# Loading pages one or two steps before their use in a fused two-block kernel

## The chip, the cores and the metric

The kernel runs on one core of a Trainium2 chip, as one program. The metric is device time in microseconds (us) of one execution, from which a median over several runs is taken. All loops are unrolled when the program is built.

## What is computed

The input is 256 tokens of width 2048 (`x`), 256 memory tokens (`mem`), 256 context tokens (`ctx`) and two conditioning vectors (`c`, `c_ctx`). Two blocks follow each other. The first block:

```
mem_n = rmsnorm(mem, mem_norm_g)
x = retention_layer(x, norm_a, w_in_a, w_mem_kv[0], w_out_a, mem_n)
kv = shared_kv(x, kv_norm_g, w_kv)
x = dilated_layer(x, norm_b, w_in_b, w_mem_kv[1], w_out_b, mem_n, kv)
x = rmsnorm(x, final_norm_g)
```

Both layers also attend to the memory through `mem_n @ w_mem_kv[layer]`. The second block has two layers, a sliding-window attention (swa) and a latent attention (mla), each with a modulation:

```
shift, scale, gate = split(silu(c) @ ada_w[i] + ada_b[i], 3)       # the same with c_ctx for ctx
h  = rmsnorm(x, norm_g[i]) * (1 + scale) + shift
hc = rmsnorm(ctx, norm_g[i]) * (1 + scale_c) + shift_c
o, oc = mixer(h, hc, ...)
x, ctx = x + gate * o, ctx + gate_c * oc
```

All arrays are float32. The change alters none of this arithmetic.

## The kernel before

**Projections.** Nearly all time goes into matrix products of 256 or 512 tokens with weight matrices. Every operand is split into a high part in the matmul's own float32 type and a low part (what the rounding left), and three products are summed: high by high, low by high, high by low. A projection (`gemm`, `gemm_T`, `gemm_wide`, `gemm_HL`) makes one block of 512 output columns (1024 in `gemm_wide`), and walks the contraction in steps `u` of four 128-row pieces. A step is one call of `wload`: a weight load of 1 MB into a `raw` buffer (four of them), a cast to `wh` on ScalarE (line 134, three buffers) and a subtraction to `wl` on VectorE (line 135, two buffers); then its matmuls (line 99) follow. `gemm_HL` fills four PSUM accumulators of the five that exist; `add_halves` evacuates them by a copy on ScalarE (line 300) and an addition on VectorE (line 301). There are 32 such evacuations.

**Side work.** Behind the matmuls of each step stand two calls. `tick()` advances every spawned generator by one `yield`: small jobs such as norms, attention chains and loads are written as generators and so spread over the steps of the projections; `later(fn, wait)` runs `fn` after `wait` more ticks, and `drain()` runs all to their end. `fill(n)` adds `n` to a credit, and for each whole credit takes the next of 96 modulation units (`ada_unit`): one load of 1 MB of `ada_w` into a `raw` buffer and eight VectorE instructions (lines 383 and 385), with a transposition and sums (388, 389) after every fourth. `FA`, `FB`, `FS` are the credits per step in the retention, dilated and swa layers; what is left before the last swa column block is done by `fill(96)`.

**Order.** All loads and stores are issued by one queue, SP (line 96). Tiles come from pools; nearly all activations live in pages of 128 by 512 float32 from one pool of 66 pages. The order of instructions on each engine is not the text's: a planner in the framework sets it when the program is built, by the text's order as priority, by its own estimate of durations, and by when buffers come free. Each engine then works through its list in that order.

**The places that the change touches.**
- `mem_rows` (line 605) loads the eight row pages of `mem` in four steps, and sums their squares (`rows`, `sumsq`, line 123); then come the reciprocal root, the conditioning vectors and a broadcast. `enter_x` (616) follows: in each of four steps it loads two transposed pages of `x`, scales them into the pages `ha` (`split_gain`, lines 319 and 320), loads two row pages and sums their squares. All this runs beside the two `gemm_HL` projections of `mem_kv(1)` (four steps each, first memory projections) and the first of `mem_kv(0)`.
- `enter_ctx` (905) does the like for `ctx`, beside the column blocks 1 to 3 of the dilated layer's output projection (six steps each), into the pages `hs`.
- The first swa projection (`kr`, line 1019) starts with two steps for the context tokens (`ahead=2`), before the latent tokens are normed, modulated and transposed by `hT_mod` (lines 895, 111, 332, 339, 340). The norm needs the last block of the output projection (additions in lines 944 and 946, small VectorE sums, a power on GpSimd in line 961).
- In the swa layer the mixed heads of the first two groups are spilled to DRAM (`mixsd`, eight pages) and brought back by `reload` (1052), spawned before the last `gemm_T`; each page is loaded into `mixSL`, cast to `mixSH` (line 325) and subtracted in place (line 326). The swa output projection `out_swa` then begins with these pages.

Of the kernel before, what the change touches and what calls it, by code (L numbers as in the profile page):

```python
# [11 lines left out]
F32 = mybir.dt.float32  # L12
# [6 lines left out]
P = 128  # L19
D = 2048  # L20
NK = D // P
# [1 line left out]
S128 = 128 ** -0.5  # L23
NPAGES = 66
NRAW = 4
FA, FB, FS = 0.25, 0.23, 0.58
NMISC = 3
MPER = 2

# [31 lines left out]
def tile_kernel(ctx: ExitStack, tc: tile.TileContext, d, out):  # L61
# [17 lines left out]
    def pg(s="pg", dt=F32, shape=None):  # L79
        return ppool.tile(shape or [P, 512], dt, name=nm(s), tag="pg")  # L80
# [14 lines left out]
    def load(dst, src):  # L95
        nc.sync.dma_start(dst, src)
# [24 lines left out]
    def sumsq(dst, src, w):  # L121
        j = spool.tile([P, 512], BF16, name=nm("junk"), tag="junk", bufs=1)
        A.activation(j[:, :w], src, AF.Square, accum_out=dst)
# [37 lines left out]
    def later(fn, wait=0):  # L161
        def gen():
            for _ in range(wait):
                yield
            fn()
            return
            yield
        spawn(gen())
# [11 lines left out]
    def gemm(act, tl, w, nkk, c0, ncols=512, nfill=0.0, order=None, pre=None, mid=False, ahead=0, apart=False):  # L180


        accs = [acc() for _ in tl]
        order = list(range(0, nkk, 4)) if order is None else order
        order = [q if isinstance(q, tuple) else (q, min(4, nkk - q)) for q in order]
        first, last = order[0][0], sum(order[-1]) - 1
        tl = [(act, t) if act else t for t in tl]
        held = {}

        def products(u, n, sel, tick_mid):  # L190
            h, l = held[u]
            for k in range(n):
                for i in sel:
                    sh, sl = tl[i][0].st(u + k, tl[i][1])
                    mm(accs[i][:, :ncols], sh, h[:, k], u == first and k == 0, False)
                    mm(accs[i][:, :ncols], sl, h[:, k], False, False)
            if tick_mid:
                tick()
            for k in range(n):
                for i in sel:  # L200
                    mm(accs[i][:, :ncols], tl[i][0].st(u + k, tl[i][1])[0], l[:, k], False, u + k == last)

        for u, n in order[:ahead]:
            held[u] = wload(w, u * P, n, c0, ncols)
            products(u, n, range(2), False)
        for i, (u, n) in enumerate(order):
            if pre:
                pre(u)
            if i < ahead:
                products(u, n, range(2, len(tl)), mid)  # L210
            else:
                held[u] = wload(w, u * P, n, c0, ncols)
                if apart and u + n == nkk:
                    for j in range(len(tl)):
                        products(u, n, [j], False)
                else:
                    products(u, n, range(len(tl)), mid)
            tick()
            fill(nfill)
        return accs  # L220
# [91 lines left out]
    def split_gain(act, kk, src, gcol, t0=0, nt=None):  # L312

        h, l = act.sl(kk) if isinstance(act, ActHL) else act.sl(kk, t0, nt)
        if gcol is None:
            A.copy(h, src)
            V.tensor_tensor(l, src, h.bitcast(F32), ALU.subtract)
        else:
            A.activation(h, src, AF.Copy, scale=gcol)
            V.scalar_tensor_tensor(l, src, gcol, h.bitcast(F32), ALU.mult, ALU.subtract)  # L320
# [28 lines left out]
    def gain(i, kk):  # L349
        return gT[:, i * NK + kk : i * NK + kk + 1]  # L350

    N_A, N_B, KV_N, MEM_N, N20, N21 = range(6)
# [226 lines left out]
    ha = new_HL("ha")  # L579
# [4 lines left out]
    def enter_page(srcT, act, gi, i):  # L584
        u = pg("natT")
        load(u, srcT[i])
        for k in range(2):
            split_gain(act, 2 * i + k, u[:, k * 256 : (k + 1) * 256], gain(gi, 2 * i + k))

    def enter(srcT, act, gi, c):  # L590
        for i in (2 * c, 2 * c + 1):
            enter_page(srcT, act, gi, i)

    def rows(src, q, c):
        for t in range(2):
            u = pg("nat")
            load(u, src[t * P : (t + 1) * P, c * 512 : (c + 1) * 512])
            sumsq(q[:, 4 * t + c : 4 * t + c + 1], u, 512)

    def row_rsqrt(dst, q):  # L600
        ssq = small(2)
# [2 lines left out]

    def mem_rows():
        q = const([P, 8], "ssm")
        for c in range(4):
            rows(d["mem"], q, c)
            yield
        row_rsqrt(memr, q)  # L610
        condition()
        yield
        bcast_rows(memrB[:, 0:256], memr)
        yield from enter_x()

    def enter_x():
        q = const([P, 8], "ssxa")
        for c in range(4):
            enter(d["xT"], ha, N_A, c)
            rows(d["x"], q, c)  # L620
            yield
        row_rsqrt(ra, q)
        V.tensor_scalar(sra, ra, 1.0 / 16.0, None, ALU.mult)
        V.tensor_scalar(hra, ra, 0.5, None, ALU.mult)
# [3 lines left out]
    def mem_kv(layer):  # L628
        kT, vn = [None] * 4, [[None] * 2 for _ in range(2)]
        w = d["w_mem_kv"][layer]  # L630
        if layer == 1:
            accs = gemm_wide(hm, w, 1024, [(0, 1), (1, 1)] + [(u, 2) for u in range(2, NK, 2)],
                             lambda u: u % 2 == 0 and enter_page(d["memT"], hm, MEM_N, u // 2))
            spawn(mem_rows())
            vs = [[pg("mkv") for _ in range(2)] for _ in range(2)]
            for c in range(2):
                for t in range(2):
                    A.copy(vs[c][t], accs[c][t])

            def post():  # L640
                for c in range(2):
                    for t in range(2):
                        A.activation(vs[c][t], vs[c][t], AF.Copy, scale=memr[:, t : t + 1])
                        load(memb[4 + 2 * t + c], vs[c][t])
            later(post, 7)
        for c in range(2):
            raw = add_halves(gemm_HL(hm, w, c * 512, FA if layer == 0 or c else 0), "mkT")

            def post(c=c, raw=raw):
                for j in range(2):  # L650
                    V.tensor_tensor(raw[j].rearrange("p (k n) -> p k n", k=2), raw[j].rearrange("p (k n) -> p k n", k=2),
                                    bc(memrB[:, 0:256], 2), ALU.mult)
                    if layer == 1:
                        load(memb[2 * c + j], raw[j])
                    else:
                        kT[2 * c + j] = split_page(raw[j], "mkTs")
            later(post, 5 if layer == 1 and c == 0 else 0)
        if layer == 0:
            for c in range(2):
                acs = gemm(hm, [0, 1], w, NK, 1024 + c * 512, nfill=FA)  # L660
                for t in range(2):
                    vn[t][c] = split_rows(acs[t], memr[:, t : t + 1])
        return kT, vn
# [27 lines left out]
    for hg in range(2):  # L691
        dec = []
        for h in range(4):
            q = pg("dec")
# [64 lines left out]
    for c in range(4):  # L759
        res = []  # L760
        for t in range(2):
            q = pg("xr")
# [125 lines left out]
    hs = new_act(NK, 512, "hs")  # L888
# [15 lines left out]

    def enter_ctx():
        q, rc = const([P, 8], "ssc"), const([P, 2], "rc")
        for c in range(4):
            rows(d["ctx_2"], q, c)
        row_rsqrt(rc, q)
        yield  # L910
        rcB = pg("rcB")
        bcast_rows(rcB[:, 0:256], rc)
        for i in range(8):
            u = pg("natT")
            load(u, d["ctxT"][i])
            V.tensor_tensor(u.rearrange("p (k n) -> p k n", k=2), u.rearrange("p (k n) -> p k n", k=2),
                            bc(rcB[:, 0:256], 2), ALU.mult)
            split_mod(hs, 2 * i, 2, u, modA[0][:, 1, 2 * i : 2 * i + 2], adaT[0][:, 2 * i : 2 * i + 2, 1])
            if i % 2:
                yield  # L920

    def splitB(u):
        if u == 12:
# [8 lines left out]
    for c in range(4):  # L932
# [3 lines left out]
        for t in range(2):  # L936
            q = pg("x1r")
# [4 lines left out]
        for t in range(2):  # L942
            q = res[t]
# [21 lines left out]
    WS = d["swa_w_in_2"]  # L965
    TL = [2, 3, 0, 1]
# [45 lines left out]
    def evac4(acs):  # L1012
        res = [None] * 4
        for i, t in enumerate(TL):
            res[t] = pg("ev")
            A.copy(res[t], acs[i])
        return res

    kr = evac4(gemm(hs, TL, WS, NK, 2048, nfill=FS,
                    pre=lambda u: hT_mod([z[0][u // 4], z[1][u // 4]], r23, 0, 0, hs, u // 4), ahead=2))  # L1020
    kn = [None] * 4
    for t in TL:
# [27 lines left out]
            mixS.H[k], mixS.L[k] = pg("mixSH", F32R), pg("mixSL", F32R)  # L1050

    def reload():
        for u in range(0, 8, 4):
            for k in range(u, u + 4):
                open_page(k)
                q = mixS.L[k].bitcast(F32)
                load(q, mixsd[k])
                split_in_place(mixS, k)
            yield

    for j in range(4):
        qr = evac4(gemm(hs, TL, WS, NK, j * 512, nfill=FS))
# [506 lines left out]
```

## Time and profile before

| | us |
|---|---|
| median of 3 runs | 3096.49 (3095.86 to 3096.86) |
| profiled execution | 3096.07 |
| its span, first to last instruction | 3094.3 |
| TensorE busy | 3042.5 (98%) |
| VectorE busy | 2163.8 (70%) |
| ScalarE busy | 1411.2 (46%) |

The profile is of one execution. Busy time of TensorE (PE) is the time in which some matmul is in flight. The granted clock of a stretch is given as a share of 2.4 GHz; 1.0 is that level and 0.5 is 1.2 GHz, so a value between them is a mixture. Idle time of an engine is listed with the instruction that ended it. A DMA's time runs from its issue on SP to its landing.

### The profile page before, as it was taken

What the parts mean: (1) busy time and instruction counts of PE and PEld (TensorE: products, weight loads), DVE (VectorE), ACT (ScalarE), POOL (GpSimd) and SP (SyncE); (2) the same over time, 40 slices, a digit from 0 to 9 for tenths busy, and PEclk for the clock granted to TensorE, in tenths of its full rate; (3) what the DMA queues carried; (4) which work ended last, traced back from release to release, by engine and by line L of the source; (5) the groups of instructions that cost most, each with busy time, mean ns of one, the idle gap of its engine ahead of it and who ended that gap; (6) DMA issues with size and microseconds to landing.
All of it is one profiled execution on the core that took longest, in us unless ns stands there. A gap on an engine that the chain in (4) does not pass through costs nothing.

```text
span 3094.3 us, 38864 instructions
## 1 busy us (share of the span) xinstructions
PE 3042.5 (98%) x15386; PEld 2570.2 (83%) x15386; DVE 2163.8 (70%) x3277; ACT 1411.2 (46%) x1870; POOL 86.2 (3%) x63
## 2 busy tenths in 40 slices
PE   9799999999999999999999999999999999999999
PEld 7688888888888888888888888788888778888887
DVE  5677877878867767766766747867676766656774
ACT  6444444445433433433433555424355342645662
POOL 0000000000000000000000000010110100000110
PEclk9899999999999999999999999999999999999999
DMA  8776676677566656656656667544433435453234
GB/s 307 242 243 226 210 245 222 221 260 264 206 208 234 232 185 227 222 195 227 231 191 227 222 224 248 181 157 156 136 118 108 163 103 180 145 176 123 69 103 129
DMA packets 307863, 600.77 MB, mean 194 GB/s; under 512 B 12896, under 2 KB 24800, under 8 KB 307680
## 3 DMA queue, kind: packets, MB, share of 16 engines
q1 hardware_dynamic: 307680, 598.29, 57.3%
q8 instruction: 120, 1.97, 0.3%
q14 instruction: 63, 0.52, 0.0%
HBM read 585.62 MB, written 12.62 MB: 193 GB/s over the span
## 4 chain that ended last, share of the span: by engine, by line
PE 92%; DVE 4%; DMA 1%; ACT 1%; POOL 1%; issue 1%; SPq 0%; DVEq 0%; ACTq 0%
PE acc L99 83%; PE pT L111 2%; PE so L99 1%; PE bs L99 1%; PE ls L99 1%; PE bo L99 1%; DMA raw<-in_ada_w 1%; DVE wl L135 1%; PE xs L99 1%; DVE ada L385 1%; PE lo L99 1%; PE mixT L111 0%; PE mo L99 0%; PE ms L99 0%; PE yT L111 0%
## 5 line engine op out<-in xcount | busy, mean ns | idle before, releaser
L135 DVE TENSOR_TENSOR wl<-raw,wh 128x2048 fp32r<-128x2048 f32 (+2 forms) x437 | 982.2, 2248 | 601.8 <-PE acc L99 343.4
L134 ACT CAST wh<-raw 128x2048 fp32r<-128x2048 f32 (+2 forms) x437 | 821.0, 1879 | 1136.3 <-PE acc L99 1021.0
L385 DVE SCALAR_TENSOR_TENSOR ada<-raw,condth,ada 128x512 f32<-128x512 f32 x720 | 496.0, 745 | 60.7 <-DMA raw<-in_ada_w 60.5
L99 PE MATMUL acc<-hb,wh 128*128 128x512 f32 x896 | 232.6, 393 | 0.0
L99 PE MATMUL acc<-wh,ha 128*128 128x512 f32 x896 | 215.2, 392 | 0.0
L99 PE MATMUL acc<-hk,wh 128*128 128x512 f32 x768 | 199.4, 394 | 0.1
L99 PEld LDWEIGHTS acc<-wh,ha 128*128 128x128 f32 x896 | 166.3, 188 | 33.5
L99 PE MATMUL acc<-wh,hk 128*128 128x512 f32 x768 | 185.3, 393 | 0.0
L99 PEld LDWEIGHTS acc<-hb,wh 128*128 128x128 f32 x896 | 159.8, 188 | 27.0 <-DVE hb L443 0.5
L99 PEld LDWEIGHTS acc<-wh,hk 128*128 128x128 f32 x768 | 143.1, 188 | 28.6
L99 PEld LDWEIGHTS acc<-hk,wh 128*128 128x128 f32 x768 | 136.7, 188 | 22.5 <-DVE bq L301 0.4
L99 PE MATMUL acc<-wh,hsH 128*128 128x512 f32 x384 | 151.2, 397 | 0.0
L99 PE MATMUL acc<-wh,hsL 128*128 128x512 f32 x384 | 150.6, 395 | 0.0
L99 PEld LDWEIGHTS acc<-hb,wl 128*128 128x128 f32 x896 | 126.1, 190 | 11.8 <-ACT hb L442 0.2
L99 PE MATMUL acc<-hb,wl 128*128 128x256 f32 x896 | 129.8, 282 | 0.0
L99 PEld LDWEIGHTS acc<-hk,wl 128*128 128x128 f32 x768 | 108.0, 190 | 10.2
L99 PE MATMUL acc<-hk,wl 128*128 128x256 f32 x768 | 110.9, 282 | 0.0
L99 PE MATMUL acc<-wl,ha 128*128 128x512 f32 x448 | 110.7, 389 | 0.0
L99 PE MATMUL acc<-wh,mixSH 128*128 128x512 f32 x256 | 101.2, 400 | 5.8 <-ACT mixSH L325 3.8
L99 PE MATMUL acc<-wh,mixSL 128*128 128x512 f32 x256 | 101.0, 400 | 2.2 <-DVE mixSL L326 2.2
L99 PE MATMUL acc<-hsH,wh 128*128 128x512 f32 x256 | 99.7, 391 | 0.0
L99 PE MATMUL acc<-hsL,wh 128*128 128x512 f32 x256 | 99.3, 390 | 0.0
(404 smaller groups left out, 5405.1 us busy)
## 6 DMA issues: line engine op xcount, KB each, us to landing
raw<-in_ada_w SPq DMA_DIRECT2D x96, 1024.0 KB, 5.1
raw<-in_w_kv SPq DMA_DIRECT2D x96, 1024.0 KB, 5.0
raw<-in_w_in_b SPq DMA_DIRECT2D x80, 1024.0 KB, 5.0
raw<-in_w_in_a SPq DMA_DIRECT2D x64, 1024.0 KB, 5.3
raw<-in_swa_w_in SPq DMA_DIRECT2D x40, 1024.0 KB, 5.0
raw<-in_w_mem_kv SPq DMA_DIRECT2D x31, 1024.0 KB, 5.3
raw<-in_w_out_a SPq DMA_DIRECT2D x24, 1024.0 KB, 5.2
raw<-in_w_out_b SPq DMA_DIRECT2D x24, 1024.0 KB, 5.2
```

Of the source, the lines that this page charges most:

```text
L99: T.matmul(o, lhsT=l, rhs=r, start=start, stop=stop)
L111: T.transpose(o, i, ident[:k, :k])
L134: A.copy(h, rw)
L135: V.tensor_tensor(l, rw, h.bitcast(F32), ALU.subtract)
L385: V.scalar_tensor_tensor(a[ci], raw[:, k, :], col, a[ci], ALU.mult, ALU.add)
```

## The change

A helper `staged(n, begin, end, lag)` runs `begin(i)` in one tick and `end(i)` `lag` ticks later, so that up to `lag` further groups are begun before a group's work. Memory and `x` are staged by two steps, the context rows by one, the context pages by two (one page per tick in place of two), the spilled pages by one (in two groups of four). `mem_rows` thereby takes two ticks more and `enter_x` two more; three waits of `later` in `mem_kv` are lengthened. `FS` becomes 0.64, and the first swa projection has no `nfill`.

```diff
-FA, FB, FS = 0.25, 0.23, 0.58
+FA, FB, FS = 0.25, 0.23, 0.64
...
+    def staged(n, begin, end, lag=2):
+
+        got = []
+        for i in range(n + lag):
+            if i < n:
+                got.append(begin(i))
+            if i >= lag:
+                end(i - lag, got[i - lag])
+            yield
...
     def mem_rows():
         q = const([P, 8], "ssm")
-        for c in range(4):
-            rows(d["mem"], q, c)
-            yield
+        yield from staged(4, lambda c: load_rows(d["mem"], c), lambda c, us: sum_rows(q, c, us))
         row_rsqrt(memr, q)
         condition()
         yield
...
     def enter_x():
         q = const([P, 8], "ssxa")
-        for c in range(4):
-            enter(d["xT"], ha, N_A, c)
-            rows(d["x"], q, c)
-            yield
+
+        def begin(c):
+            return [load_page(d["xT"][i]) for i in (2 * c, 2 * c + 1)], load_rows(d["x"], c)
+
+        def end(c, got):
+            for i in range(2):
+                for k in range(2):
+                    split_gain(ha, 4 * c + 2 * i + k, got[0][i][:, k * 256 : (k + 1) * 256], gain(N_A, 4 * c + 2 * i + k))
+            sum_rows(q, c, got[1])
+        yield from staged(4, begin, end)
...
-            later(post, 7)
+            later(post, 8)
...
-            later(post, 5 if layer == 1 and c == 0 else 0)
+            later(post, (6, 3)[c] if layer == 1 else 0)
...
     def enter_ctx():
         q, rc = const([P, 8], "ssc"), const([P, 2], "rc")
-        for c in range(4):
-            rows(d["ctx_2"], q, c)
+        yield from staged(4, lambda c: load_rows(d["ctx_2"], c), lambda c, us: sum_rows(q, c, us), 1)
         row_rsqrt(rc, q)
         yield
         rcB = pg("rcB")
         bcast_rows(rcB[:, 0:256], rc)
-        for i in range(8):
-            u = pg("natT")
-            load(u, d["ctxT"][i])
+
+        def end(i, u):
             V.tensor_tensor(u.rearrange("p (k n) -> p k n", k=2), u.rearrange("p (k n) -> p k n", k=2),
                             bc(rcB[:, 0:256], 2), ALU.mult)
             split_mod(hs, 2 * i, 2, u, modA[0][:, 1, 2 * i : 2 * i + 2], adaT[0][:, 2 * i : 2 * i + 2, 1])
-            if i % 2:
-                yield
+        yield from staged(8, lambda i: load_page(d["ctxT"][i]), end)
...
-    kr = evac4(gemm(hs, TL, WS, NK, 2048, nfill=FS,
+    kr = evac4(gemm(hs, TL, WS, NK, 2048,
...
     def reload():
-        for u in range(0, 8, 4):
-            for k in range(u, u + 4):
+        def begin(i):
+            for k in range(4 * i, 4 * i + 4):
                 open_page(k)
-                q = mixS.L[k].bitcast(F32)
-                load(q, mixsd[k])
+                load(mixS.L[k].bitcast(F32), mixsd[k])
+
+        def end(i, _):
+            for k in range(4 * i, 4 * i + 4):
                 split_in_place(mixS, k)
-            yield
+        yield from staged(2, begin, end, 1)
```

The new helpers `load_rows`, `sum_rows` and `load_page` are the old `rows` and `enter_page` cut into their load and their work.

## Rows read from the trace of the kernel before

**Rows 1.** The page's first part: busy us (share of span) and instructions of TensorE.
```profile
PE 3042.5 (98%) x15386; PEld 2570.2 (83%) x15386; DVE 2163.8 (70%) x3277; ACT 1411.2 (46%) x1870; POOL 86.2 (3%) x63
```

**Rows 2.** Waits of TensorE, whole span: us in total, times, longest.
```profile
PE acc L99 <- DVE mkT L301: 16.6, 1, 16.6
...
PE acc L99 <- ACT mixSH L325: 3.8, 1, 3.8
PE yT L111 <- ACT y L895: 3.7, 2, 3.4
...
PE acc L99 <- DVE mixSL L326: 2.2, 2, 1.4
PE acc L99 <- ACT mixSH L316: 1.8, 1, 1.8
```

**Rows 3.** Chain of waits, 80 to 125 us: start, us, what.
```profile
101.36 5.31 DVE ada L385 x8
...
107.66 6.67 DMA nat<-in_x
...
118.00 0.35 DVE mkT L301
```

**Rows 4.** Timeline of ScalarE there: start, us, instruction [idle before it <- releaser].
```profile
106.29 0.63 ACT L123 ACTIVATE junk<-nat 128x512 bf16<-128x512 f32 x1 [5.44 <-DMA nat<-in_x]
...
117.39 1.16 ACT L300 COPY mkT<-acc 128x256 f32<-128x256 f32 x4
```

**Rows 5.** Timeline of TensorE there: the blocks of high products after the stop.
```profile
118.48 2.04 PE L99 MATMUL acc<-hm,wh 128*128 128x512 f32 x4 [16.56 <-DVE mkT L301]
...
121.18 1.91 PE L99 MATMUL acc<-hm,wh 128*128 128x512 f32 x4
...
123.52 1.08 PE L99 MATMUL acc<-hm,wh 128*128 128x512 f32 x4
...
124.92 2.91 PE L99 MATMUL acc<-hm,wh 128*128 128x512 f32 x12
```

**Rows 6.** Windows: us, busy of PE, PEld, DVE, ACT, POOL; clock, DMA share, GB/s.
```profile
86.00:99.00 13.00, 13.00 (x76) 11.41 (x76) 7.68 (x7) 4.62 (x6) 0.00 (x0) 1.00 1.00 368
99.00:118.50 19.50, 2.94 (x18) 2.09 (x16) 11.32 (x21) 9.05 (x24) 0.00 (x0) 0.68 0.80 271
```

**Rows 7.** Timeline of TensorE, 1922 to 1943 us.
```profile
1923.12 1.98 PE L99 MATMUL acc<-wl,mixBH 128*128 128x512 f32 x8
...
1939.65 0.69 PE L111 MATMUL yT<-ident,y 128*128 128x128 f32 x2 [3.44 <-ACT y L895]
...
1942.63 0.39 PE L99 MATMUL acc<-wh,hsH 128*128 128x512 f32 x1
```

**Rows 8.** Chain of waits, 1895 to 1955 us.
```profile
1914.44 10.14 DMA raw<-in_ada_w
...
1928.01 1.20 DVE x1r L944 x2
```

**Rows 9.** The tile `mixSL`, its loads: issue ns min/median/max, first and last start.
```profile
L96 SPq DMA_DIRECT2D mixSL<-mixsd x8: 423/476/1534, 2424.6 to 2453.6; - x8
```

**Rows 10.** Timeline of TensorE, 2445 to 2550 us.
```profile
2450.09 0.39 PE L99 MATMUL acc<-wh,mixSH 128*128 128x512 f32 x1
...
2460.14 0.50 PE L99 MATMUL acc<-wh,mixSH 128*128 128x512 f32 x1 [3.80 <-ACT mixSH L325]
...
2468.08 0.45 PE L99 MATMUL acc<-wh,mixSH 128*128 128x512 f32 x1
```

**Rows 11.** Timeline of ScalarE, 2445 to 2550 us.
```profile
2459.47 1.21 ACT L325 CAST mixSH<-mixSL 128x512 fp32r<-128x512 f32 x2 [3.17 <-DMA mixSL<-mixsd]
...
2462.51 0.59 ACT L1105 ACTIVATE cp<-cs,sm,rss 128x256 f32<-128x256 f32 x1
```

**Rows 12.** The tile `natT` between 1840 and 1925 us, its loads.
```profile
L96 SPq DMA_DIRECT2D natT<-in_ctxT x8: 450/497/563, 1844.7 to 1892.8; - x8
```

**Rows 13.** A window over most of the swa layer; columns as in rows 6.
```profile
1960.00:2440.00 480.00, 479.54 (x2250) 393.06 (x2249) 340.76 (x660) 202.64 (x342) 36.95 (x20) 1.00 0.42 139
```

More of the change, by code (lines that the diff above doesn't have):

```diff
@@ L588, in enter_page, with load_rows, sum_rows, load_page @@
             split_gain(act, 2 * i + k, u[:, k * 256 : (k + 1) * 256], gain(gi, 2 * i + k))
[L590 to L594, printed above, removed]
-        for t in range(2):
-            u = pg("nat")
-            load(u, src[t * P : (t + 1) * P, c * 512 : (c + 1) * 512])
-            sumsq(q[:, 4 * t + c : 4 * t + c + 1], u, 512)
+    def staged(n, begin, end, lag=2):
[6 more added lines that the diff above has]
+            yield
+    def load_rows(src, c):
+        us = [pg("nat") for _ in range(2)]
+        for t in range(2):
+            load(us[t], src[t * P : (t + 1) * P, c * 512 : (c + 1) * 512])
+        return us
+    def sum_rows(q, c, us):
+        for t in range(2):
+            sumsq(q[:, 4 * t + c : 4 * t + c + 1], us[t], 512)
+    def load_page(src):
+        u = pg("natT")
+        load(u, src)
+        return u
     def row_rsqrt(dst, q):
```

## Prediction, on record before the changed kernel was run

> **What bounds the kernel now.** I read the page first: TensorE (PE) is busy 3042.5 of 3094.3 us [rows 1], so only its 52 idle us, and stretches in which it runs at half its clock, can be won without removing matmuls; this change removes none. Next the list of what PE waited for [rows 2]. It names single places: 16.6 us once for a VectorE (DVE) evacuation `mkT`, 3.8 + 2.2 us for `mixSH`/`mixSL`, 3.4 us for `y`, and 1.8 us for a later `mixSH`. The reader is to see that these are not averages but four events. For each I then read the chain of waits, the timeline of the engines, and the windows around it.
>
> *Place 1, at 101 us* (first memory projections). The chain [rows 3] runs: DVE does eight modulation instructions until 106.67; only then does a weight load on SP get its buffer, and the loads of the `x` pages stand behind it on SP; one of them takes 107.66 to 114.33; `mkT` is evacuated at 118.00. ScalarE (ACT) shows why [rows 4]: the sum over an `x` page sat in its queue waiting 5.44 us for the load, and the four PSUM copies (L300) that PE needs came after, at 117.39. PE restarts at 118.48 with the clock down: a block of four high and four low products takes 2.70, then 2.34, then 1.40 us again [rows 5]; the granted clock of 99 to 118.5 us is 0.68 [rows 6], which mixes the 1.2 and 2.4 GHz levels. Price: 16.56 idle + (2.70 - 1.40) + (2.34 - 1.40) = 18.8 us.
>
> *Place 2, at 1936 us* (entry of the swa layer). PE finished the matmuls of the output projection at 1923.12 + 1.98 = 1925.1, worked ahead, and then stood 3.44 us until 1939.65 for `y` [rows 7]. The chain [rows 8] begins with a modulation load of 10.14 us from 1914.44; DVE worked on it, and the addition L944, whose inputs PE had ready at 1925.1, started at 1928.01. From 1939.65 to 1942.63 PE ran slow (2.98 us); at the ratio 1.40/2.70 of place 1 that is 1.4 us too much. Price: 4.9 us.
>
> *Place 3, at 2456 us* (first swa output projection). The eight spilled pages are loaded from 2424.6 to 2453.6, 4.1 us apart on the mean, though issuing one takes 0.48 us [rows 9]. PE starts the projection at 2450.09 and runs out of pages [rows 10]; ACT waits for the last loads until 2459.47 [rows 11]. Idle 6.0 us [rows 2]; and of 2460.14 to 2468.08, less the 2.2 idle inside, 5.7 us pass at the low clock, 2.8 too many. Price: 8.8 us.
>
> **The change part by part.**
>
> *x pages* (16 loads, 16 ACT scalings, 16 DVE subtractions, 8 sums). In the old text the work on a page stands directly behind its load, and the next load behind that. The planner gives pages out in the order of the text; I infer this from the loads, which alternate with the work on the page before, here and in [rows 9, 12]. The new text puts three groups of four loads in front of the first work, and, as `x` now begins two steps later, the evacuation L300/L301 that PE needs is in front of all work on `x`. So the queue of [rows 4] is turned round: L300 can go at about 98 us, when its sums are done, and place 1 loses its cause. What is late next: the same 4.19 MB now arrive while the next projection runs. That stretch, four steps of four blocks of 1.40 us, is 22.4 us; it wants 4.2 MB of weights, 4.19 MB of `x` and a modulation load of 1.05 MB, 9.4 MB, 25.6 us at the 368 GB/s that moved with all queues busy [rows 6]. Short by 3.2 us, which I charge to PE: gain 15.6. Bounds: 18.8 if the four prefetched weight buffers cover it; -1.5 if everything queues, 11.4 us of transfer plus one latency of 6.7 [rows 3], against the 16.6 of today. I stay near the upper end, because the evacuation itself no longer waits for a load.
>
> The DMA page of the Trainium skill ("DMA: Bandwidth & Descriptors", Specifications) speaks against the change here: it gives a core about 358 GB/s of HBM, so loading earlier makes no room. The trace shows 368 GB/s, 3% more, in the 13 us in front of the stall, so it agrees that this is the ceiling. By the page's figure the shortfall would be 4.0 instead of 3.2 us; its stronger form is the first rival below.
>
> *Memory pages* (8 loads, 8 sums) and the three delays of `later`. [Rows 2] has no PE wait for a memory page: gain 0. The delayed instructions are stores to DRAM read a layer later, and two scalings; if this cover failed it would show as one page latency, 6.7 us.
>
> *Context pages* (8 row loads and sums, 8 pages). They take 48 us today, 1844.7 to 1892.8, 6.9 us each [rows 12], and PE waits for none of them [rows 2]: gain 0. In the new text the last one stands in step 16 of the 18 that the remaining three column blocks have; its margin is two steps, about 12 us (24 matmuls of 1.98/8 us each, [rows 7]). If the margin fails, PE waits one page, 6.9 us. I take 0: the loads run two ahead, and the first two steps of the swa projection need only the first half of these pages.
>
> *No modulation work in the first swa projection, FS 0.64.* Four of 48 fills of 0.58 go, 2.3 units; the other 44, at 0.64, give the same sum (28.2 units against 27.8). Gone from place 2 are two loads on SP and the DVE work on them. Then L944 starts at 1925.1; even if all 11.6 us between L944 and the first transpose stayed (1928.01 to 1939.65), `y` would be there at 1936.7, and PE runs dry at 1936.2: 0.5 us is left. Part of the 11.6 is modulation work itself, so I take 4.5 of the 4.9; bounds 0 and 4.9. The moved 2.3 units cost DVE 5.31 us each [rows 3], 12.2 us over 44 steps, 0.28 per step. Cover: DVE is busy 341 of 480 us there, PE 479.5 [rows 13]. I take 0; 12.2 if it were all exposed.
>
> *Spilled pages.* Eight loads now stand together ahead of any cast. From 2424.6, eight issues of 0.48 and one latency of 6.7 end at 2435; eight casts of 0.6 us [rows 11] end near 2440, ten us ahead of PE at 2450.09. Place 3 goes, 8.8 us. What is late next: the attention of the last head group, whose exponential stood behind these casts at 2462.51 [rows 11] and for which PE waits 1.83 us later on [rows 2]. It moves up by the wait and casts in front of it, 3.17 + 1.21 = 4.4, while PE moves up 8.8. So up to 4.4 can come back; I take half, and a gain of 6.6. Bounds 0 (the loads keep their times) and 10.6.
>
> **Sum.** 15.6 + 4.5 + 6.6 = 26.7 us. The profiled execution took 3096.07 us (1.8 outside its span), 0.4 below the median of 3096.49; 3096.07 - 26.7 = 3069.4, against the median 3069.8. I forecast 3069.5.
>
> **Rivals.**
> - *Place 1 only moves.* The burst of loads fills the DMA, ACT and DVE wait in order on pages, weight casts stand behind them, and PE stops in the next projection. For: all queues busy at 86 to 99 us [rows 6]. Against: evacuation is out of the way. Then 3069.4 + 15.6 = 3085.
> - *The attention sets the pace at place 3.* The gain of 6.6 is given back: 3076. For: PE already waits for it for 1.8 us [rows 2].
> - *The loads keep their times*, because free pages or SP's weight loads and not the text hold them. Only place 2 gains: 3096.1 - 4.5 = 3091.6, inside the noise bound. For: the `x` loads of [rows 3] came when SP got past a weight load. Against: the even spacing of [rows 9, 12].
> - *Slower: late evacuations elsewhere.* The planner orders everything after 60 us anew. The kernel has 32 projections with the evacuation of L300/L301; one of them stalls today. Each new one of that kind costs 18.8 us; the sign turns at the second (26.7/18.8 = 1.4), and two make 3069.4 + 37.6 = 3107. For: the planner put one evacuation behind a load that the chip delivers later. Against: elsewhere no page loads stand in front of evacuations, and 31 of 32 are clean [rows 2].
>
> **Chances.** Forecast 0.63, with its own range 3062 to 3077; place 1 moves 0.13; attention 0.09; loads keep their times 0.06; slower 0.05; still more than forecast (all upper ends, 34 us) 0.04. A change under 0.2%, 6.2 us, can't be told from none here. Faster 0.63 + 0.13 + 0.09 + 0.04 = 0.89; within 0.2% 0.06; slower 0.05. The range 3060 to 3086 holds the forecast and two rivals.
>
> **What would show it.** Right: PE's waits have no `mkT` L301; L300 of that projection near 98 us; no modulation load between 1900 and 1950 and no PE wait for `y`; the eight `mixSL` loads within some 10 us and no wait for L325. Wrong: an ACT or DVE wait for `nat` or `natT` with a PE wait for `wh` or `wl` behind it at 105 to 130 us; `mixSL` loads still spread over 29 us; a longer wait for L316.

## The result

The changed kernel takes 3067.19 us (median of 4 runs, 3066.27 to 3068.69) against 3096.68 (4 runs, 3095.86 to 3097.73): ratio 0.9905, 95% interval 0.9888 to 0.9922. That is 29.5 us faster; 27.0 were forecast (3069.5 against 3096.49).

The page after, its first part. The busy times are those of [rows 1] within 8 us; what went is idle time of TensorE (PE), 52 us before and 30 now, and time at the low clock.

```profile
PE 3035.0 (99%) x15386; PEld 2564.1 (84%) x15386; DVE 2159.2 (70%) x3277; ACT 1410.7 (46%) x1870; POOL 87.8 (3%) x63
```

To place the gain I took the first matmul of each stage in the two traces. Each length runs to the next stage's first matmul. For `ha` it is the first one in the form `acc<-wh,ha`, in the retention layer's second projection; the layer's first projection starts 22.3 us earlier in both traces, so the changes are the same.

```
stage (its first tile)               before     after    change
start to the retention layer (ha)     227.6     210.3     -17.3   place 1
ha to hb                              497.6     497.6       0.0
hb to mixBH                          1055.5    1056.8      +1.3
mixBH to hsH (dilated output)         144.2     143.1      -1.1   beside the ctx pages
hsH to mixSH (swa projections)        525.2     521.1      -4.1   place 2
mixSH to hlH (swa output)             215.8     207.6      -8.2   place 3
hlH to the end                        428.4     428.7      +0.3
span                                 3094.3    3065.2     -29.1
```

The waits of PE after, the answer to [rows 2]. The 16.6 for `mkT` has become 1.8, L325 and L326 are gone, `y` is down to 0.2. New are small waits for `pTs`, `hb` and `hsH`.

```profile
PE acc L99 <- DVE mkT L301: 1.8, 1, 1.8
PE xs L99 <- DVE pTs L456: 1.2, 1, 1.2
...
PE acc L99 <- DVE hb L443: 1.0, 1, 1.0
PE acc L99 <- DVE hsH L339: 1.0, 1, 1.0
PE pT L111 <- DVE pTs L456: 0.8, 1, 0.8
...
PE acc L99 <- ACT mixSH L316: 0.5, 1, 0.5
...
PE yT L111 <- ACT y L914: 0.2, 1, 0.2
```

*Place 1.* ScalarE (ACT) after, to be held against [rows 4]: the four copies come first, and the sum that waits for an `x` page stands behind them.

```profile
99.50 1.20 ACT L300 COPY mkT<-acc 128x256 f32<-128x256 f32 x4
102.04 0.63 ACT L123 ACTIVATE junk<-nat 128x512 bf16<-128x512 f32 x1 [1.35 <-DMA nat<-in_x]
```

VectorE (DVE) there. In front of the addition L301 stand modulation work and a scaling; DVE waits for nothing.

```profile
99.64 0.75 DVE L385 SCALAR_TENSOR_TENSOR ada<-raw,condth,ada 128x512 f32<-128x512 f32 x1
100.31 1.29 DVE L670 TENSOR_TENSOR mkT<-mkT,memrB 128x512 f32<-128x512 f32 x2
101.52 1.41 DVE L385 SCALAR_TENSOR_TENSOR ada<-raw,condth,ada 128x512 f32<-128x512 f32 x2
102.84 1.41 DVE L301 TENSOR_TENSOR mkT<-acc,mkT 128x256 f32<-128x256 f32 x4
```

PE there, the answer to [rows 5]: 1.85 us of idle time, and the block behind it takes 1.16, not 2.04; the clock did not fall.

```profile
100.46 1.09 PE L99 MATMUL acc<-hm,wh 128*128 128x512 f32 x4
103.40 1.16 PE L99 MATMUL acc<-hm,wh 128*128 128x512 f32 x4 [1.85 <-DVE mkT L301]
```

The stretch of [rows 6] after (us, busy of PE, PEld, DVE, ACT, POOL, granted clock, DMA share, GB/s): clock 1.00 in place of 0.68, and 380 GB/s in place of 271.

```profile
99.00:118.50 19.50, 17.65 (x101) 15.21 (x101) 18.98 (x32) 14.36 (x36) 0.00 (x0) 1.00 1.04 380
```

*Place 2.* PE at the first transposes after: nothing to wait for, where [rows 7] has 3.44 us.

```profile
1916.83 1.98 PE L99 MATMUL acc<-wl,hsH 128*128 128x512 f32 x8
1918.65 1.03 PE L111 MATMUL yT<-ident,y 128*128 128x128 f32 x8
```

Some 3 us later PE does stop, 0.98 us for `hsH`. The chain of waits there begins with a modulation load again:

```profile
1911.25 5.99 DMA raw<-in_ada_w
...
1917.27 4.06 DVE ada L385 x6
1921.33 0.21 DVE hsH L339
```

*Place 3.* The loads of `mixSL` after, the answer to [rows 9]: 4.8 us from the first to the last, not 29, and 20 us ahead of PE, which starts on these pages at 2428.9.

```profile
L96 SPq DMA_DIRECT2D mixSL<-mixsd x8: 320/410/629, 2403.8 to 2408.6; - x8
```

The chain of waits later in that stage shows what is late now: the attention's `pTs` (its probabilities, transposed), behind modulation work that stands behind a modulation load.

```profile
2456.13 6.84 DMA raw<-in_ada_w
...
2463.00 1.42 DVE ada L385 x2
...
2465.22 0.60 DVE pTs L456
...
2465.86 2.36 PE xs L99 x9
```

### The profile page after: what moved, and what is told of

Same layout as the page of the kernel before. It is cut to its first block, busy times and chain, and to the rows that moved or that the text cites. A ratio compares the mean times of both kernels' runs of the same rounds, so it can differ in the third digit from the quotient of the medians.

```text
span 3065.2 us, 38873 instructions
## 1 busy us (share of the span) xinstructions
PE 3035.0 (99%) x15386; PEld 2564.1 (84%) x15386; DVE 2159.2 (70%) x3277; ACT 1410.7 (46%) x1870; POOL 87.8 (3%) x63
## 4 chain that ended last, share of the span: by engine, by line
PE 92%; DVE 4%; DMA 2%; ACT 1%; POOL 1%; issue 0%; SPq 0%; DVEq 0%; ACTq 0%
PE acc L99 82%; PE pT L111 1%; DMA raw<-in_ada_w 1%; DVE wl L135 1%; PE bs L99 1%; PE bo L99 1%; PE so L99 1%; DVE ada L385 1%; PE ls L99 1%; PE xs L99 1%; PE lo L99 1%; PE mixT L111 0%; POOL sm L119 0%; PE mo L99 0%; PE ms L99 0%
## 5 line engine op out<-in xcount | busy, mean ns | idle before, releaser
L385 DVE SCALAR_TENSOR_TENSOR ada<-raw,condth,ada 128x512 f32<-128x512 f32 x720 | 498.1, 745 | 74.4 <-DMA raw<-in_ada_w 74.1
```

The source lines that it names most:

```text
L385: V.scalar_tensor_tensor(a[ci], raw[:, k, :], col, a[ci], ALU.mult, ALU.add)
```

## The experiments

### Each part alone

Four kernels, each with one part of the change on the kernel before: `x_only` (`mem_rows`, `enter_x`, the three waits of `later`), `fill_only` (FS 0.64 and no `nfill` in the first swa projection), `reload_only`, `ctx_only`.

> The kernel before with only the staging of the memory and x pages and the three longer waits of later; the rest is old. My theory (each part acts in its own place): PE's 16.6 us wait for mkT L301 shrinks to about 2 us, the half-clock stretch behind it goes, -17 us, 3079 to 3080; places 2 and 3 keep their waits for y (3.4) and mixSH/mixSL (6.0). Rival (the four parts need each other, since the planner orders everything anew): the gain is under 12 us, or the later waits change by more than 2 us.

> The kernel before with only FS 0.64 and no fill in the first swa projection. My theory: PE's wait for y (3.4 us) goes with its slow stretch, -4 to -5 us, 3092; place 3 keeps its 6 us. Rival (the modulation unit in front of mixSL on VectorE is what held place 3, and moving the units shifts it): place 3 loses over 3 us of its wait as well and the run is at 3087 or less. Second rival (the wait for y was due to late x1r loads behind the context pages): y is still waited for and the run is within 1.5 us of before.

> The kernel before with only the staged reload of the spilled pages. My theory (pages are handed out in the text's order, so a cast between two loads makes the second wait for the first): the eight mixSL loads go out within 5 to 6 us instead of 29, PE's waits for L325 and L326 (6.0 us) go, -7 to -9 us, 3088 to 3090. Rival (SP's weight loads or full pages space the loads): they stay spread over more than 15 us and the gain is under 3 us.

> The kernel before with only the staged context rows and pages. My theory: nothing waits for them, 3095.5 to 3097.5, and PE's wait for y stays at 3 to 4 us. Rival (the additions L944 of the last block waited for x1r loads that stood behind the context pages, so this part and not the fill is what freed place 2): the wait for y falls under 1 us and the run is at 3092 to 3093.

Measured, with the change in the three stages that matter (by the first matmuls, as above):

```
             median us   ratio, 95% interval        to ha   hsH to mixSH   mixSH to hlH
x_only       3079.43     0.9940 [0.9923, 0.9956]    -17.1     +0.1           +0.2
fill_only    3090.73     0.9976 [0.9966, 0.9986]     -1.1     -4.6           -2.2
reload_only  3087.94     0.9969 [0.9957, 0.9980]     -0.6     +1.1          -10.7
ctx_only     3093.13     0.9987 [0.9977, 0.9996]     +0.2     -3.1           -0.4
all four     3067.19     0.9905 [0.9888, 0.9922]    -17.3     -4.1           -8.2
```

`x_only` and `reload_only` act at their own places and within or next to the times expected. `fill_only` came out 1.3 us below the 3092 expected; it also gains 2.2 us at place 3, which was to keep its waits: PE's wait for L316 there falls from 1.8 to 0.5. The gains don't add up: the four spans alone gain 37.8 us, together 29.1. At place 2 the two parts that gain 4.6 and 3.1 alone gain 4.1 together, since both shorten the same stop; at place 3 the reload alone gains 10.7 and the whole 8.2.

That `ctx_only` gains at place 2 I had not expected. What follows is read from the traces; no run changes the order on SP alone. In the kernel before, SP issues the first modulation load at 1914.44, and the addition of the last output block follows at 1928.01 [rows 8]. With the context pages alone changed, SP issues it here (SP's queue: start, us):

```profile
1911.64 0.38 SPq L96 DMA_DIRECT2D raw<-in_ada_w  x1
```

and DVE reaches that addition (L966 in this kernel) 2.4 us earlier; PE's wait for `y` falls from 3.44 to 1.39:

```profile
1925.63 1.27 DVE L966 TENSOR_TENSOR x1r<-acc,x1r 128x512 f32<-128x512 f32 x2
```

A second small gain of this part is the stage before: a wait of 1.0 us for the broadcast `rB` of the context rows at 1846.67 is gone there, and in the changed kernel. It stands in the whole list of [rows 2]:

```profile
PE rB L99 <- DVE dg L569: 1.0, 1, 1.0
```

### Place 1: loads ahead, or work later?

The change does two things to `x`: its loads stand two steps ahead of the work, and its work stands later. `x_late` has the old body, two steps later (and the three longer waits of `later`); `x_early` has staged loads and the old start.

```diff
 # x_late: old enter_x, begun two ticks later
+        yield
+        yield
         bcast_rows(memrB[:, 0:256], memr)
         yield from enter_x()
```

```diff
 # x_early: mem_rows and later() as before
     def enter_x():
...
+        yield from staged(4, begin, end)
```

> The old body of enter_x (load two pages, work on them, load the next), begun two ticks later, so that all but the first group stands behind the evacuation L300/L301. My theory: what counts is that no work waiting for an x page stands in front of the evacuation on ScalarE and VectorE; the planned order still has four scalings of the first two x pages ahead of L300, and two ada instructions and four subtractions ahead of L301, so a part of the stall stays: a wait for mkT of 4 to 9 us instead of 16.6, 3085 to 3090 us, and the x pages, loaded two by two, may cost a wait for ha later. Rival 1, position alone does it: 3080 as with staged loads, wait for mkT under 2.5. Rival 2, only loads ahead of the work count: 3097, wait for mkT near 16.

> Before, with the x pages staged two steps ahead, but begun at the old step (memory rows as before): loads ahead of the work as in the change, work where x_late had it. x_late kept 13.7 us of waits for mkT in two places, each behind a load that was late. My theory now: the loads ahead are what counts, since then work that stands in front of an evacuation finds its page there; so at place 1 the wait for mkT falls to 2 to 4 us (four scalings, four subtractions and three sums are planned ahead of L300/L301, some 3 us of work), 3081 to 3084 us. Rival, both are needed (loads ahead and the later step): a load stays late in front of the evacuation, wait over 6 us, 3088 or more. Second rival, the step does not matter at all: 3079.4 as with both, wait 1.7.

`x_late`: 3096.97 us, ratio 0.9999 [0.9989, 1.0008]; nothing is gained. My number was wrong by 7 to 12 us, and the rival's time is the one that came, by another way than it said. PE's waits in `x_late`:

```profile
PE acc L99 <- DVE mkT L301: 13.7, 2, 7.0
```

The one stop has become two, and at each ACT shows a scaling of an `x` page whose load is late, with the copies behind it.

```profile
106.59 0.91 ACT L319 ACTIVATE ha<-natT,gT 128x256 fp32r<-128x256 f32 x2 [5.49 <-DMA natT<-in_xT]
107.40 1.17 ACT L300 COPY mkT<-acc 128x256 f32<-128x256 f32 x4
...
137.61 0.91 ACT L319 ACTIVATE ha<-natT,gT 128x256 fp32r<-128x256 f32 x2 [4.67 <-DMA natT<-in_xT]
138.42 1.17 ACT L300 COPY mkT<-acc 128x256 f32<-128x256 f32 x4
```

But modulation work stands in front of L301 as well. At the first stop DVE is busy without a gap until 107.1 and does these five last, at the second eight behind a load of 7.35 us:

```profile
103.72 3.39 DVE L385 SCALAR_TENSOR_TENSOR ada<-raw,condth,ada 128x512 f32<-128x512 f32 x5
```

So the late pages alone do not decide either stop: at the first one L301, which started at 107.93, could not have gone before 107.1 in this order without them either. The two causes are not separated.

`x_early`: 3081.2 us, ratio 0.9948 [0.9931, 0.9964], within the range expected; PE's waits for `mkT` are 0.67 and 0.50, shorter than the 2 to 4 expected, and the stage up to `ha` takes 210.8 us, as good as with both. Four scalings do stand in front of the copies, but they find their pages there:

```profile
100.24 1.70 ACT L319 ACTIVATE ha<-natT,gT 128x256 fp32r<-128x256 f32 x4
101.85 1.16 ACT L300 COPY mkT<-acc 128x256 f32<-128x256 f32 x4
```

So the loads ahead give all but 0.3 us of the gain at place 1, and the later step alone gained nothing in the order that the planner made of it.

### Place 1: was there room in the DMA?

```diff
 # x_twice, on the changed kernel: each x page loaded a second time, never read
+            for i in (2 * c, 2 * c + 1):
+                load_page(d["xT"][i])
+            load_rows(d["x"], c)
```

> The changed kernel with every x page loaded a second time into a page that nobody reads: 16 more loads, 4.19 MB, 11.4 us of transfer at 368 GB/s, in front of the weight load that follows the x pages on SP. It measures how much room the DMA had at place 1, for which the prediction charged 3.2 us. If the DMA was at its limit there, all 11.4 us come out as a wait of TensorE for weights: 3078 to 3080 us. My theory: there was room, some 4 to 6 us of prefetched weights, and the wait for wh is 5 to 8 us: 3072 to 3076. Rival, much room: under 2 us, 3067 to 3069.

3078.55 us, ratio 0.9940 [0.9925, 0.9955]: 11.4 us more than the changed kernel, as much as the added transfer takes. My number was wrong; the time of the first alternative came, though not as a wait for weights alone. PE, timeline:

```profile
105.42 2.05 PE L99 MATMUL acc<-hm,wh 128*128 128x512 f32 x4 [4.30 <-DVE mkT L301]
...
132.04 2.50 PE L99 MATMUL acc<-hm,wh 128*128 128x512 f32 x5 [6.29 <-ACT wh L134]
```

PE is idle 6.29 us for `wh` and 2.45 us longer at `mkT` than in the changed kernel. That is 8.7 us; the rest fits the low clock behind both stops (the first block takes 2.05 against 1.16). At `mkT` six modulation instructions, until 104.9, stand in front of L301. At `wh` PE waits for a cast that stands on ACT behind the split of an `mkT` page:

```profile
129.57 0.62 ACT L455 CAST mkTs<-mkT 128x512 fp32r<-128x512 f32 x1 [1.81 <-DVE mkT L674]
130.10 1.89 ACT L134 CAST wh<-raw 128x2048 fp32r<-128x2048 f32 x1
```

The load of these weights went out at 120.59 and landed 8.0 us later, at 128.6. In the changed kernel it goes out at 109.61 and lands 7.1 us later, at 116.7, and its cast begins at 119.80 with no wait for it. So there was room there, some 3 us. That the whole cost equals the added transfer is the sum of these stops, and does not show that the DMA had nothing over.

### Place 1: the last 1.85 us

```diff
 # after_c1_nofill: no modulation in the second projection of mem_kv(1)
-gemm_HL(hm, w, c * 512, FA if layer == 0 or c else 0)
+gemm_HL(hm, w, c * 512, FA if layer == 0 else 0)
 # cand: nor in the first of mem_kv(0); FS 0.58
+gemm_HL(hm, w, c * 512, FA if layer == 0 and c else 0)
```

> The changed kernel without modulation work in the second half of the first memory projection too (four credits of 0.25, one unit, are done later). My theory: the 1.85 us that TensorE still waits for mkT at 103.4 come from ada instructions in front of L301 on VectorE; without them it waits under 0.5, and the time is 1.5 to 2.5 us less than the changed kernel: 3065. Rival (the wait is for the copies or for SP, busy with x loads): the wait stays near 1.8 and the time at 3067. Second rival: the unit that moved falls in front of another evacuation and costs 1 to 3 us there.

3066.66 us, ratio 0.9899 [0.9885, 0.9914]: no different from the changed kernel, and 1.7 more than the 3065 expected. The wait fell to 1.13 only. The edit took out the unit ahead of the one that is in the way: a unit of the next projection is placed here, two of its L383 and one L385 in front of L301 again. Besides, a wait of 1.25 for `wh` appeared at 123.36, and the stage up to `ha` takes 211.7 us, 1.4 more than in the changed kernel.

```profile
101.57 0.48 DVE L383 TENSOR_SCALAR ada<-raw,condth 128x512 f32<-128x512 f32 x1
101.97 0.75 DVE L385 SCALAR_TENSOR_TENSOR ada<-raw,condth,ada 128x512 f32<-128x512 f32 x1
102.63 1.41 DVE L301 TENSOR_TENSOR mkT<-acc,mkT 128x256 f32<-128x256 f32 x4
```

> The changed kernel with FS 0.58 and without modulation work in the three memory projections up to the first of the retention layer's two; the planned order has no ada instruction in front of L301 at place 1 or in the projection after it. The run without the unit in the second projection alone had left two ada instructions in front of L301 (the unit of the next projection moved up), and a wait of 1.1. Theory (ada in front of L301 makes the wait of 1.85): wait under 0.5, the stage up to the retention layer's projections 1.5 to 2 us shorter than 210.0, and 3061.5 to 3062.5 in all. Rival (the scaling L670 with its wait for the broadcast, or the copies, are late anyway): wait 0.8 to 1.2, stage 209 to 211, 3063 to 3064.

3070.33 us, ratio 0.9914 [0.9899, 0.9929], where 3061.5 to 3062.5 were expected. Its first half held: no modulation instruction stands there, L301 starts at 101.34, no wait for `mkT` is left, and `ha` is reached at 208.9, 1.1 us earlier than with FS 0.58 alone (below; 1.5 to 2 were expected). But five units were left for the burst before the last swa column block, and PE waited for their sums; the swa output stage takes 214.5 us, 10.8 more than with FS 0.58 alone:

```profile
2594.03 0.34 PE L99 MATMUL adaT<-adar,s 128*32 128x32 f32 x8 [4.85 <-DVE adar L389]
```

### Place 3: order of the loads, and what is late next

```diff
 # reload_grouped, on the kernel before: the new begin and end, lag 0
+        yield from staged(2, begin, end, 0)
 # after_fs58, on the changed kernel
-FA, FB, FS = 0.25, 0.23, 0.64
+FA, FB, FS = 0.25, 0.23, 0.58
```

> Before, with the spilled pages loaded four at a time and then cast four at a time in the same tick (no step ahead); the planned order on SP then has the loads in two groups of four in place of single loads between casts. My theory (pages are handed out in the order of the text, a load behind a cast waits for that cast): the loads fall into two bursts of four within some 2.5 us each, the second behind the casts of the first, some 10 to 12 us later; the last lands near 2445 to 2448, the waits for L325 and L326 shrink from 3.8 + 2.2 to under 2, and the gain is 6 to 9 us: 3088 to 3091. Rival (it is the earlier tick that counts, not the order): loads still spread to 2450 or later, 3095 to 3097.

3088.63 us, ratio 0.9970 [0.9959, 0.9981]. Four loads before four casts, in the same step, do nearly all that the step ahead does (3087.94). The loads of `reload_grouped` and, below it, of `reload_only`:

```profile
L96 SPq DMA_DIRECT2D mixSL<-mixsd x8: 377/440/593, 2428.0 to 2437.0; - x8
```

```profile
L96 SPq DMA_DIRECT2D mixSL<-mixsd x8: 319/423/646, 2425.0 to 2429.9; - x8
```

Against [rows 9] nothing moved but the order of loads and casts, and the loads went from 29 us to 9 (two groups of four, at 2428.0 and 2435.3). So the order in the text decides. That the planner does it by handing out pages in that order fits, but was not tested by itself.

> The changed kernel with FS 0.58 in place of 0.64, still without modulation work in the first swa projection; 2.6 units fall to the rest before the last swa column block. My theory: at place 3 the changed kernel gained 8.2 against 10.7 for the reload part alone, because a modulation unit whose load came late (raw at 2463.0) stands in front of pTs L456 on VectorE; another rate moves that unit, so the waits for pTs (1.2 + 0.8) go and the first output projection of swa takes 205 to 206 in place of 207.6 us. The leftover of 2.6 units is done behind the attention and may cost up to 2 us there. Net 3064 to 3068. Rival (the rate does not matter, the loss comes from the earlier place): the stage keeps 207.6 us and the time is 3067 to 3070.

3063.52 us, ratio 0.9889 [0.9872, 0.9905]; 3.7 us less than the changed kernel, and below the range expected. The swa output stage takes 203.7 in place of 207.6 us, and PE's wait for `pTs` in this kernel is

```profile
PE xs L99 <- DVE pTs L456: 0.4, 1, 0.4
```

That is 1.6 us less than the 1.2 and 0.8 of the changed kernel in this stage. The reason that I had given, that the rate moves the unit away, is not confirmed: a modulation unit whose load came late stands in front of `pTs` here too, though only two of its instructions do in place of three:

```profile
2461.98 0.75 DVE L385 SCALAR_TENSOR_TENSOR ada<-raw,condth,ada 128x512 f32<-128x512 f32 x1 [2.03 <-DMA raw<-in_ada_w]
```

The other 2.3 us of the stage are spread over several places, and their cause stays open. The burst here has three units, and PE does not wait for it. The swa projections take 1.4 us more than with 0.64 (522.5 against 521.1), and the dilated layer 1.1 less (1055.7 against 1056.8), where FS has no part.

### A last version

```diff
 # cand2: cand with FA 0.27, so that the retention layer takes up the two units
+FA, FB, FS = 0.27, 0.23, 0.58
```

> The changed kernel with FS 0.58, without modulation work in the memory projections up to the first of the retention layer's two, and FA 0.27 in place of 0.25, so that the retention layer does the two units that these projections did; from the swa layer on the units stand as with FS 0.58 alone (three instead of five in the burst before the last swa column block). Theory: the run without this correction gained 1.1 us at place 1 and lost it to the burst (TensorE waited 4.85 us for the last modulation sums at 2594); with three units that wait goes, place 1 keeps its gain, and the time is 3062 to 3063. Rival (the rate 0.27 puts units in front of evacuations in the retention layer): 3064 to 3067, with waits there; second rival (the burst of loads, not its count, was late): the wait for adaT stays near 4.8, 3069 or more.

3063.29 us, ratio 0.9892 [0.9876, 0.9909]: not to be told from `after_fs58`. Both waits went (`mkT` and `adaT`), but the denser units put others into the retention layer:

```profile
PE acc L99 <- DVE gs L450: 2.8, 3, 1.6
```

Its 1.9 us more from `ha` to `mixaH` than in `after_fs58` (361.7 against 359.8) outweigh the 0.9 us by which it reaches `ha` earlier. Both versions are some 3.8 us (0.12%) below the changed kernel. The intervals of the ratios to before overlap; the times themselves (3062.42 to 3063.94 and 3062.22 to 3065.96, against 3066.27 to 3068.69) and the stage of the swa output do not.

## Why the prediction was right, and where it was not

- *Sum.* Forecast 26.7 (15.6 + 4.5 + 6.6); measured 29.1 in the span. All three places lost the stop that the prediction named, and none of the rivals came: no wait for `wh` behind `x` at place 1, no longer wait for L316, no new stalled evacuation, and the loads did not keep their times. Two of the signs it gave failed: 1.85 us for `mkT` are left, and modulation loads still go out between 1900 and 1950. That the sum came so near is in part luck: the terms below miss on both sides, and at place 3 one miss of 5.5 us and one of 3.9 partly cancel.
- *x pages, 15.6: the charge of 3.2 us for the DMA was mis-sized.* Place 1 gained 17.3 of its 18.8. What is missing, 1.5, is about the stop of 1.85 behind modulation work on DVE; `cand`, without that work, has none, and reaches `ha` 1.4 us earlier. The wait for `wh` that was charged did not come. Two inputs of the charge were off. Loads go out from 94.6, ahead of the projection whose 22.4 us were to hold them, and the ceiling is above 368: 380 GB/s over 19.5 us. The Trainium skill's page "DMA: Bandwidth & Descriptors" (Specifications) gives about 358 GB/s of HBM per core; this trace goes 6% over it, so the measurement stands. The direction of the warning was right all the same: 4.19 MB more in this stretch (`x_twice`) cost 11.4 us.
- *The reason given for place 1 was half wrong.* The prediction stressed that the evacuation comes in front of all work on `x`, because `x` begins later. `x_early` (not later, 16.8 of 17.1) shows that the staged loads do it without the later step. `x_late` (later, gain 0) fits that, but modulation work stood in front of its evacuations too.
- *Memory pages, 0.* Not separated; `x_early` without them and `x_only` with them differ by 0.3 us up to `ha`. Their medians are 1.8 us apart, but of the 1.5 between the two spans 1.4 come after `hlH`, where neither part acts.
- *Context pages, 0: wrong.* Alone they gain 4.3 us by medians: 3.1 at place 2, where SP comes to the modulation load 2.8 us earlier, and 1.0 for `rB`. The prediction looked only for PE waits on the pages themselves, and passed over the wait for `rB`, which belongs to this part, and what is queued behind the loads on SP. In the whole the gain at place 2 is hidden, because the other part shortens the same stop; the one for `rB` stays (1.1 us in the table).
- *No modulation work in the first swa projection, 4.5.* Alone 4.6, in the whole 4.1. The sign to look for, no modulation load between 1900 and 1950, failed: loads go out at 1911.25 and 1938.20, as later units moved up, and the work on the first makes PE wait 0.98 us for `hsH`.
- *FS 0.64, cost 0: wrong by 3.9 us at place 3*, or 2.5 net of the 1.4 that the projections gain from it. The prediction added up DVE time per step; what it left out is that the rate also sets where the units stand among the attention's work. Of the 3.9 us 1.6 are waits for `pTs`; the rest is open. It is no cost of the rate as such: in the old kernel the same rate, with the fill gone, gains 2.2 us at this place.
- *Spilled pages, 6.6: mis-sized.* Measured 8.2; 10.7 alone, at the upper bound of 10.6; with FS 0.58 in the changed kernel 12.1, above it. The 2.2 that the attention was to give back did not come: the wait for L316 fell from 1.8 to 1.0 in `reload_only` and to 0.5 in the whole. The price of 8.8 also left out that PE ran at the low clock for 3.2 us behind that wait (rows in the last section); in the changed kernel the clock is 1.00 over this stage. What took back a part in the changed kernel are new waits, among them 2.0 us for `pTs`.
- *Not accounted for:* +1.3 us in the dilated layer, with a wait of 1.0 for `hb`. `reload_grouped`, which changes nothing there, has one of 1.2, and `after_fs58` has none, so it goes with the planner's new order; its cause stays open.

## What to carry to other kernels

Where work in order waits for a load, first look whether the loads stand ahead of all the work in the text; moving load and work together to a later step gained nothing here. Before loading ahead, add up the bytes of the stretch against what the DMA moves there: here 4.19 MB fitted in without a stop of TensorE for a load, and as much again cost 11.4 us. When a stop is removed, the next one comes from whatever side work now happens to stand in front, so its rate is worth trying at two or three values.

## What the runs showed of the hardware

At place 1 TensorE's clock fell behind longer stops only: after idle times of 0.67 (`x_early`) and 1.85 us the next block of four took 1.16 us at a granted clock of 1.00, after 4.30 (`x_twice`) and 6.67 (`x_late`) it took 2.05 and 2.04 at 0.50, the 1.2 GHz level. But the length of the one stop does not settle it: in the kernel before, a stop of 1.83 us in the swa output stage was followed by 3.2 us at 0.50 (PE; below it the window, with the columns of [rows 6]). What made the difference is not shown.

```profile
2515.40 0.76 PE L99 MATMUL acc<-wh,mixSH 128*128 128x512 f32 x2 [1.83 <-ACT mixSH L316]
```

```profile
2516.10:2519.30 3.20, 3.20 (x14) 2.88 (x13) 0.54 (x2) 1.84 (x4) 0.00 (x0) 0.50 0.01 3
```

And page and weight loads issued back to back by one queue, with a few stores among them, moved 380 GB/s over 19.5 us (379 over 33 us in `x_twice`), more than the 368 that I had taken as the ceiling.
